# Loading the first chunk tile by tile in the order of use, with wider warming products

## The chip, the cores and the metric

One core of one Trainium2 chip runs the kernel once per measurement. The metric is the device time of one execution in microseconds (us), as the median of several runs; smaller is better. All times below that are given with a start count from the first instruction of the profiled execution.

## The reference

One transformer block on x of 256 rows and 1024 features, all in 32-bit floats. What matters here is its beginning:

```
h    = rms_norm(x, norm_mix_g)             # x: 256 x 1024
proj = h @ w_in                            # 1024 x 2048: k, q, v and u of 512 columns each
k, q = rope(rms_norm(k, g)), rope(rms_norm(q, g))
x    = x + concat(pool(u), attention(q, k, v)) @ w_out
x    = x + cross_attention(norm(x), norm(mem)) @ ...     # reads mem, 256 x 1024
x    = x + conv_ffn(norm(x))                             # w_up 1024 x 5632, w_down 2816 x 1024
```

## The kernel before

x lies transposed on the chip: eight tiles (k = 0 to 7) of 128 features x 256 rows, in the tile `sc` (columns C_X on; `resid` is a view of them). All weights come through one stream, `wpack`, in chunks of 128 x 2048 floats (1 MB). A chunk holds two units of 1024 columns, and a ring of three buffers `raw` takes the chunks in turn. In the first part each unit holds two 512-column weight tiles, so that chunk 0 (called W0 below) has the weights of k = 0 to 3 of the first product, chunk 1 (W1) those of k = 4 to 7; W2 and W3 hold the next product (q), W4 and W5 the one after it (v), and so on. The first block of `wpack`, W0, is stored so that each quarter of 512 columns is contiguous in memory; of W1 and later chunks each partition has a row of 8 KB, and a load of some columns takes a piece of every row. x is stored as one contiguous block for each load (`FIRST_X` lists the cuts).

Every product is made of three passes on TensorE, because each number is split in a high part (float32r, a rounding by ACT or DVE) and a low part (the rest, by DVE): `wh` and `wl` of the weights (L207, L218), `xg` high and low of the scaled x (L268, L274). `a_chunk` runs k = 0 to 7 for one product of 512 columns: for each k, two matmuls of 512 columns at L408 (high x, high weight), two at L410 (low x, high weight) and two at L413 (high x, low weight). `first_splits` writes out by hand the order of the splits for the first product:

```
for k in range(KT):
    if k == 2: split_h(k // 2, r)                      # weight's high part first
    part_h(xgv[0][:, k], resid[:, k], col(sc, C_GMIX + k))
    if k != 2: split_h(k // 2, r, dve.tensor_copy if k == 0 else act.copy)
    part_l(...); split_l(...)
```

Engines work off their instructions in the order in which the program gives them. Later units are split by `need`, some units ahead of TensorE; `loads_to` issues a chunk's load on SP's queue when the buffer that it takes (the one of three chunks before) has been read by the last split of it, DVE's `wl`. Between these, by hand-tuned numbers of waiting steps (the WAIT lists), jobs place the rest: squares of x and their sum (`sqx`, `accx`), rope of k and q (L425 to L457), the transposes of k and q (L489, L493), scores (L567), softmax (L596), the pool branch (L682 to L685). The eight matmuls at L366, before all this, multiply zeros into a PSUM bank that nobody reads; they are the warming products.

The first loads are issued on SP's queue, but for the first half of W0, which is issued on ACT's. The loads share eight semaphores in rotation: from the ninth load on, the issuing queue waits for the landing of the load eight places before.

Of the kernel before, what the change touches and what calls it, by code (L numbers as in the profile page):

```python
# [9 lines left out]
F32 = mybir.dt.float32  # L10
F32R = mybir.dt.float32r
# [5 lines left out]
P = 128  # L17
D = 1024
S = 256
KT = D // P  # L20
# [47 lines left out]


C_GMIX, C_X = 0, KT  # L70
FIRST_X = [0] + [C_X + k * S for k in (1, 2, 4, 6, 8)]
FIRST_W = [0, 512, 1024, 1536, 2048]
C_GMEM, C_GX, C_GFFN = (C_X + KT * S + 8 * i for i in range(3))
C_GXQ = C_GFFN + KT
# [13 lines left out]
def block_kernel(ctx: ExitStack, tc: tile.TileContext, wpack: bass.AP, xpack: bass.AP, scal: bass.AP,  # L88
                 memT: bass.AP, table: bass.AP, out: bass.AP):
    nc = tc.nc  # L90
    pe, act, dve, pool = nc.tensor, nc.scalar, nc.vector, nc.gpsimd
# [11 lines left out]
    def bank():  # L103
        turn[0] += 1
        return psum.tile([P, 512], F32, name=f"bank{turn[0]}", tag="bank", bufs=8)
# [59 lines left out]
    def block(flat, lo, hi):  # L165

        return flat[P * lo:P * hi].rearrange("(p n) -> p n", p=P)

    def load_chunk(c, cuts=(0, 2 * UNIT), queue=nc.sync):
        raw[c] = wring.tile([P, 2 * UNIT], F32, name=f"raw{c}", tag="raw", bufs=RAW)  # L170
        for lo, hi in zip(cuts, cuts[1:]):
            load_part(c, lo, hi, queue)
        next_load[0] = c + 1

    def load_part(c, lo, hi, queue=nc.sync):
        src = wpack[c, :, lo:hi]
        if c == 0:
            src = block(wpack[c].rearrange("p n -> (p n)"), lo, hi)
        queue.dma_start(raw[c][:, lo:hi], src)
# [19 lines left out]
    def split_h(u, r=slice(0, UNIT), copy=act.copy):  # L199
        if u // 2 == MISC:  # L200
            for j in range(2 * (u % 2), 2 * (u % 2) + 2):
                misc[j] = maskr[:, 2 * P:] if j == 2 else t2(f"misc{j}", F32R)
                act.copy(misc[j], unit(u)[:, 512 * (j % 2):512 * (j % 2) + 512])
            return
        if u not in split:
            split[u] = [wring.tile([P, UNIT], F32R, name=f"wh{u}", tag="wh", bufs=LOOK + 3), None]
        copy(split[u][0][:, r], unit(u)[:, r])  # L207

    def split_l(u, r=slice(0, UNIT)):
        if u // 2 == MISC:  # L210
            if u % 2 == 1:
                misc["l"] = t2("misc_l", F32R)
                dve.tensor_tensor(misc["l"], unit(u)[:, 512:], misc[3].bitcast(F32), op=ALU.subtract)
            return
        if split[u][1] is None:
            split[u][1] = wring.tile([P, UNIT], F32R, name=f"wl{u}", tag="wl", bufs=LOOK + 2)
        h, l = split[u]
        dve.tensor_tensor(l[:, r], unit(u)[:, r], h[:, r].bitcast(F32), op=ALU.subtract)  # L218
# [45 lines left out]
    def part_h(h, src, scale=None):  # L264
        if scale is None:
            act.copy(h, src)
        else:
            act.activation(h, src, AF.Copy, scale=scale)  # L268

    def part_l(l, src, h, scale=None):  # L270
        if scale is None:
            dve.tensor_tensor(l, src, h.bitcast(F32), op=ALU.subtract)
        else:
            dve.scalar_tensor_tensor(l, src, scale, h.bitcast(F32), op0=ALU.mult, op1=ALU.subtract)  # L274
# [28 lines left out]
    def col(t, c):  # L303
        return t[:, c:c + 1]
# [53 lines left out]
    def load_x(lo, hi):  # L358
        r = slice(C_X + lo * S if lo else 0, C_X + hi * S)
        nc.sync.dma_start(sc[:, r], block(xpack, r.start, r.stop))  # L360

    ones = nc.const_aps.tensor(1.0, (P, 1), F32)
    idle = nc.const_aps.tensor(0.0, (P, P), F32)
    warm = bank()
    for _ in range(WARM):
        pe.matmul(warm[:, 0:P], idle, idle, start=True, stop=True)  # L366

    load_x(0, 1)
    load_chunk(0, (0, 512), nc.scalar)
    load_part(0, 512, 1024, nc.scalar)  # L370
    load_x(1, 2)
    load_part(0, 1024, 1536)
    load_x(2, 4)
    load_part(0, 1536, 2048)
    load_x(4, 6)
    load_chunk(1, (0, 1024))
    load_x(6, 8)
    load_part(1, 1024, 2048)
    load_chunk(2, (0, 1024, 2048))
    nc.sync.dma_start(tab, table)  # L380
    nc.sync.dma_start(sc[:, C_GMEM:], scal)
# [2 lines left out]
    def first_splits():  # L384
        for k in range(KT):
            r = slice(k % 2 * 512, k % 2 * 512 + 512)

            if k == 2:
                split_h(k // 2, r)
            part_h(xgv[0][:, k], resid[:, k], col(sc, C_GMIX + k))  # L390
            if k != 2:
                split_h(k // 2, r, dve.tensor_copy if k == 0 else act.copy)
            part_l(xgv[1][:, k], resid[:, k], xgv[0][:, k], col(sc, C_GMIX + k))
            split_l(k // 2, r)
        next_split[0] = FIRST

    first_splits()

    def a_chunk(u0, actv, bk, *first):
# [746 lines left out]
```

## Time and profile before

| | |
|---|---|
| median of 3 runs (lowest, highest) | 381.89 us (381.72, 381.90) |
| the profiled execution's own time | 382.99 us |
| its span, first to last instruction | 381.2 us |
| PE, DVE, ACT, POOL busy | 376.5, 315.1, 246.8, 67.8 us |
| mean granted TensorE clock | 0.999 |

The profiled execution takes 1.1 us more than the median of the others, and 1.8 us of its time lie around the span. PE's 376.5 us are the times that its matmuls cover; they overlap in the pipeline, so a busy PE need not be at its fastest. A row of the timeline gives start, length, engine, line, what is written from what, and in brackets the idle time before with what ended it; "PEld" is the weight load of TensorE.

### The profile page before, as it was taken

The page shows a single profiled execution, that of the slowest core. Times are in us where ns is not written, and L with a number is a line of the kernel's source. Part 1 is how long each engine was busy: PE and PEld are TensorE (multiplying, and loading weights), DVE is VectorE, ACT ScalarE, POOL GpSimd, SP SyncE. Part 2 cuts the span into 40 slices and gives each one's busy share as a digit, 9 for nine tenths or more (in the row PEclk, how much of TensorE's full clock was granted, in tenths as well). Part 3 has the DMA queues.
Part 4 walks back from the last instruction along what each step waited for, and adds up shares of the span by engine and source line. Part 5 has one row for each costly group of instructions (what it writes and reads, how often), then busy time and mean ns, then how long its engine had stood idle before and what let it go on. Part 6 is the DMA issues. An engine that isn't in the chain of part 4 may idle for free.

```text
span 381.2 us, 6011 instructions
## 1 busy us (share of the span) xinstructions
PE 376.5 (99%) x2194; PEld 328.6 (86%) x2194; DVE 315.1 (83%) x570; ACT 246.8 (65%) x471; POOL 67.8 (18%) x148
## 2 busy tenths in 40 slices
PE   9999999999999999999999999999999999999996
PEld 7788888888888988898888888888888888888896
DVE  4689999979878859778979999999999998654460
ACT  5766878976557655845655588778877777442210
POOL 0252885142831212100220000000000000000000
PEclk9999999999999999999999999999999999999999
DMA  8996382453506635352536155665555654374500
GB/s 263 422 369 223 111 329 67 170 208 119 216 0 220 222 110 209 123 222 111 179 124 251 55 181 208 221 219 200 179 192 207 219 168 165 124 249 157 200 15 28
DMA packets 12412, 69.13 MB, mean 181 GB/s; under 512 B 1376, under 2 KB 2784, under 8 KB 4832
## 3 DMA queue, kind: packets, MB, share of 16 engines
q1 hardware_dynamic: 12096, 68.24, 49.9%
q10 hardware_dynamic: 288, 0.52, 0.4%
q8 instruction: 17, 0.28, 0.3%
q14 instruction: 11, 0.09, 0.1%
HBM read 67.71 MB, written 1.05 MB: 180 GB/s over the span
## 4 chain that ended last, share of the span: by engine, by line
PE 86%; DVE 5%; DMA 4%; POOL 2%; ACT 1%; issue 1%; ACTq 0%; DVEq 0%
PE bank L301 42%; PE bank L300 22%; PE bank L408 4%; PE bank L413 4%; PE bank L410 4%; DMA raw<-wpack 4%; DVE wl L218 2%; PE bank L285 2%; PE bank L283 2%; PE bank L284 2%; PE bank L606 1%; PE bank L567 1%; PE bank L738 0%; PE bank L876 0%; POOL rs1t L248 0%
## 5 line engine op out<-in xcount | busy, mean ns | idle before, releaser
L218 DVE TENSOR_TENSOR wl<-raw,wh 128x1024 fp32r<-128x1024 f32 (+1 forms) x127 | 151.0, 1205 | 4.5 <-ACT wh L207 4.3
L207 ACT CAST wh<-raw 128x1024 fp32r<-128x1024 f32 (+1 forms) x125 | 126.1, 1028 | 39.1 <-DMA raw<-wpack 24.1
L301 PE MATMUL bank<-hs,wh 128*128 128x512 f32 x304 | 105.4, 391 | 0.0
L300 PE MATMUL bank<-hs,wl 128*128 128x256 f32 x304 | 85.2, 280 | 0.0
L301 PEld LDWEIGHTS bank<-hs,wh 128*128 128x128 f32 x304 | 56.9, 187 | 12.4
L300 PEld LDWEIGHTS bank<-hs,wl 128*128 128x128 f32 x304 | 57.5, 189 | 0.0
L301 PE MATMUL bank<-act,wh 128*128 128x512 f32 x154 | 53.4, 391 | 0.0
L300 PE MATMUL bank<-act,wl 128*128 128x256 f32 x154 | 43.1, 280 | 0.0
L991 ACT ACTIVATE y<-up,sc 128x256 f32<-128x256 f32 x44 | 26.2, 602 | 22.3 <-DVE up L978 17.8
L301 PE MATMUL bank<-h,wh 128*128 128x512 f32 x112 | 39.4, 394 | 0.0
L998 DVE SCALAR_TENSOR_TENSOR y<-up,sc,y 128x255 f32<-128x255 f32 (+1 forms) x88 | 37.0, 494 | 0.0
L301 PEld LDWEIGHTS bank<-act,wh 128*128 128x128 f32 x154 | 28.8, 187 | 6.3
L300 PE MATMUL bank<-h,wl 128*128 128x256 f32 x112 | 31.8, 284 | 0.0
L300 PEld LDWEIGHTS bank<-act,wl 128*128 128x128 f32 x154 | 29.1, 189 | 0.0
L1045 DVE TENSOR_TENSOR o<-bank,sc 128x256 f32<-128x256 f32 x8 | 3.4, 425 | 28.3 <-PE bank L301 22.4
L301 PEld LDWEIGHTS bank<-h,wh 128*128 128x128 f32 x112 | 21.0, 188 | 4.5
L301 PE MATMUL bank<-cat,wh 128*128 128x512 f32 x62 | 21.8, 393 | 0.0
L301 PE MATMUL bank<-ox,wh 128*128 128x512 f32 x62 | 21.6, 394 | 0.0
L268 ACT ACTIVATE h<-sc 128x256 fp32r<-128x256 f32 x16 | 8.2, 510 | 20.3 <-DVE sc L784 20.2
L300 PEld LDWEIGHTS bank<-h,wl 128*128 128x128 f32 x112 | 21.2, 189 | 0.0
L408 PE MATMUL bank<-wh,xg 128*128 128x512 f32 x64 | 20.4, 400 | 0.5 <-ACT wh L207 0.5
L408 PE MATMUL bank<-wh,mg 128*128 128x512 f32 x64 | 20.6, 403 | 0.0
(249 smaller groups left out, 718.3 us busy)
## 6 DMA issues: line engine op xcount, KB each, us to landing
raw<-wpack SPq DMA_DIRECT2D x59, 1024.0 KB, 4.8
raw<-wpack SPq DMA_DIRECT2D x4, 512.0 KB, 7.9
mraw<-memT SPq DMA_DIRECT2D x4, 256.0 KB, 8.2
out<-o SPq DMA_DIRECT2D x8, 128.0 KB, 1.9
sc<-xpack SPq DMA_DIRECT2D x3, 256.0 KB, 4.9
raw<-wpack ACTq DMA_DIRECT2D x2, 256.0 KB, 3.4
raw<-wpack SPq DMA_DIRECT2D x2, 256.0 KB, 4.4
tab<-table SPq DMA_DIRECT2D x1, 480.0 KB, 9.3
```

The lines of the kernel that those rows point to most:

```text
L207: copy(split[u][0][:, r], unit(u)[:, r])
L218: dve.tensor_tensor(l[:, r], unit(u)[:, r], h[:, r].bitcast(F32), op=ALU.subtract)
L268: act.activation(h, src, AF.Copy, scale=scale)
L283: pe.matmul(o, stat[0], mov[0], start=start, stop=False)
L284: pe.matmul(o, stat[0], mov[1], start=False, stop=False)
L300: pe.matmul(b[:, 0:n], stat[1], mov[:, 0:n], start=start, stop=False, skip_group_check=not wide_first)
L301: pe.matmul(b, stat[0], mov, start=False, stop=stop, skip_group_check=not wide_first)
L408: pe.matmul(bk[tt], a[tt][0], wv[0], start=k == 0, stop=False)
L410: pe.matmul(bk[tt], a[tt][1], wv[0], start=False, stop=False)
L413: pe.matmul(bk[tt], a[tt][0], wv[1], start=False, stop=k == KT - 1)
L991: act.activation(y[:, g * S:(g + 1) * S], src[:, g * S:(g + 1) * S], AF.Identity, bias=col(sc, C_CB + f), scale=col(sc, C_CW + 2 * 2 * NFF ...
L998: dve.scalar_tensor_tensor(yy[:, j:], uu[:, :S - j], col(sc, C_CW + (2 - j) * 2 * NFF + f), yy[:, j:], op0=ALU.mult, op1=ALU.add)
```

## The change

The x tiles 2 to 7, which came in three loads of two tiles, come in six loads of one tile. W1, which came in two loads of 1024 columns, comes in four of 512. The loads of x and W1 alternate in the order in which the first product uses them. For k = 3, as for k = 2 before, ACT makes the weight's high part ahead of x's. The warming products become 512 columns wide and float32r, where they were 128 columns of float32; there are eight of them as before.

```diff
-FIRST_X = [0] + [C_X + k * S for k in (1, 2, 4, 6, 8)]
+FIRST_X = [0] + [C_X + k * S for k in range(1, KT + 1)]
...
-    idle = nc.const_aps.tensor(0.0, (P, P), F32)
+    idle = nc.const_aps.tensor(0.0, (P, 512), F32).bitcast(F32R)
     warm = bank()
     for _ in range(WARM):
-        pe.matmul(warm[:, 0:P], idle, idle, start=True, stop=True)
+        pe.matmul(warm, idle[:, 0:P], idle, start=True, stop=True)
 
     load_x(0, 1)
     load_chunk(0, (0, 512), nc.scalar)
     load_part(0, 512, 1024, nc.scalar)
     load_x(1, 2)
     load_part(0, 1024, 1536)
-    load_x(2, 4)
+    load_x(2, 3)
     load_part(0, 1536, 2048)
-    load_x(4, 6)
-    load_chunk(1, (0, 1024))
-    load_x(6, 8)
-    load_part(1, 1024, 2048)
+    load_x(3, 4)
+    load_x(4, 5)
+    load_chunk(1, (0, 512))
+    load_x(5, 6)
+    load_part(1, 512, 1024)
+    load_x(6, 7)
+    load_part(1, 1024, 1536)
+    load_x(7, 8)
+    load_part(1, 1536, 2048)
     load_chunk(2, (0, 1024, 2048))
...
-            if k == 2:
+            if k in (2, 3):
                 split_h(k // 2, r)
             part_h(xgv[0][:, k], resid[:, k], col(sc, C_GMIX + k))
-            if k != 2:
+            if k not in (2, 3):
                 split_h(k // 2, r, dve.tensor_copy if k == 0 else act.copy)
```

SP's queue from the third x load on, before (`sc<-xpack` is x, `raw_88` W0, `raw_96` W1, `raw_100` W2, `raw_157` W3; in brackets the semaphores that the issue waits for, DMAHW0 to 7 being the eight that rotate):

```order
L360 DMA sc<-xpack 128x512
L179 DMA raw_88<-wpack 128x512
L360 DMA sc<-xpack 128x512
L179 DMA raw_96<-wpack 128x1024 [waits DMAHW0_49]
L360 DMA sc<-xpack 128x512 [waits DMAHW1_49]
L179 DMA raw_96<-wpack 128x1024 [waits DMAHW2_49]
L179 DMA raw_100<-wpack 128x1024 [waits DMAHW3_49]
L179 DMA raw_100<-wpack 128x1024 [waits DMAHW4_49]
L380 DMA tab<-table 128x960 [waits DMAHW5_49]
L381 DMA sc<-scal 128x208 [waits DMAHW6_49]
L179 DMA raw_157<-wpack 128x2048 [waits DMAHW7_49,DVE_49]
```

The same place after the change (`raw_97` is W1, `raw_105` W2):

```order
L360 DMA sc<-xpack 128x256
L179 DMA raw_88<-wpack 128x512
L360 DMA sc<-xpack 128x256
L360 DMA sc<-xpack 128x256 [waits DMAHW0_49]
L179 DMA raw_97<-wpack 128x512 [waits DMAHW1_49]
L360 DMA sc<-xpack 128x256 [waits DMAHW2_49]
L179 DMA raw_97<-wpack 128x512 [waits DMAHW3_49]
L360 DMA sc<-xpack 128x256 [waits DMAHW4_49]
L179 DMA raw_97<-wpack 128x512 [waits DMAHW5_49]
L360 DMA sc<-xpack 128x256 [waits DMAHW6_49]
L179 DMA raw_97<-wpack 128x512 [waits DMAHW7_49]
L179 DMA raw_105<-wpack 128x1024 [waits DMAHW0_49]
```

Five more loads stand ahead of W2 and W3 on SP's queue. They carry the same bytes, and W2, the tables and W3 follow in the order in which they stood.

ACT's queue at the first splits (`xg` is the high part of an x tile, `wh` that of a weight tile), the difference:

```order
 L268 ACTIVATE xg<-sc 128x256 x2
-L207 CAST wh_107<-raw_88 128x512
-L207 CAST wh_116<-raw_88 128x512
+L207 CAST wh_112<-raw_88 128x512
+L207 CAST wh_121<-raw_88 128x512
+L268 ACTIVATE xg<-sc 128x256
+L207 CAST wh_121<-raw_88 128x512
 L268 ACTIVATE xg<-sc 128x256 x2
-L207 CAST wh_116<-raw_88 128x512
+L207 CAST wh_132<-raw_97 128x512
```

Only the splits of k = 3 change places there; DVE's and PE's instructions keep their order.

## Rows read from the trace of the kernel before

**Rows 1.** The page: busy times, and the chain that ended last.
```profile
PE 376.5 (99%) x2194; PEld 328.6 (86%) x2194; DVE 315.1 (83%) x570; ACT 246.8 (65%) x471; POOL 67.8 (18%) x148
PE 86%; DVE 5%; DMA 4%; POOL 2%; ACT 1%; issue 1%; ACTq 0%; DVEq 0%
```

**Rows 2.** Timeline, PE, first product (x2: two matmuls in the row).
```profile
4.42 0.80 PE L408 MATMUL bank<-wh,xg 128*128 128x512 f32 x2
5.07 0.63 PE L410 MATMUL bank<-wh,xg 128*128 128x512 f32 x2
5.53 0.62 PE L413 MATMUL bank<-wl,xg 128*128 128x512 f32 x2
...
9.85 0.61 PE L413 MATMUL bank<-wl,xg 128*128 128x512 f32 x2
10.96 0.74 PE L408 MATMUL bank<-wh,xg 128*128 128x512 f32 x2 [0.49 <-ACT wh L207]
...
16.57 0.61 PE L408 MATMUL bank<-wh,xg 128*128 128x512 f32 x2
```

**Rows 3.** The chain of work up to 110 us, in order of time: start, length, what.
```profile
3.84 6.42 DMA raw<-wpack
10.29 0.63 ACT wh L207
10.96 0.74 PE bank L408 x2
...
14.92 0.45 PE bank L413 x2
...
21.73 1.49 DVE wl L218
...
45.53 1.23 DVE wl L218
46.77 6.72 DMA raw<-wpack
```

**Rows 4.** Timeline, ACT: its first wait for W3.
```profile
18.77 1.05 ACT L207 CAST wh<-raw 128x1024 fp32r<-128x1024 f32 x1 [1.58 <-DMA raw<-wpack]
20.65 1.99 ACT L207 CAST wh<-raw 128x1024 fp32r<-128x1024 f32 x2
```

**Rows 5.** Timeline, DVE.
```profile
19.85 1.68 DVE L218 TENSOR_TENSOR wl<-raw,wh 128x1024 fp32r<-128x1024 f32 x1 [2.46 <-ACT wh L207]
21.72 1.49 DVE L218 TENSOR_TENSOR wl<-raw,wh 128x1024 fp32r<-128x1024 f32 x1 [0.19 <-PE bank L410]
```

**Rows 6.** Busy time by stretch: us, PE, PEld, DVE, ACT, POOL busy, PE's clock, DMA share, GB/s.
```profile
21.70:46.70 25.00, 25.00 (x122) 20.93 (x121) 24.16 (x44) 17.59 (x30) 12.92 (x28) 1.00 0.61 227
46.70:54.60 7.90, 7.90 (x46) 6.34 (x45) 7.83 (x14) 5.60 (x12) 6.86 (x17) 1.00 0.84 309
```

**Rows 7.** Timeline, PE and its weight loads, where PE waits again.
```profile
47.52 0.41 PEld L567 LDWEIGHTS bank<-qkT 64*128 64x128 f32 x6 [0.36 <-ACT mg L268]
57.13 0.28 PE L684 MATMUL bank<-maskr,uh 128*128 128x256 f32 x1
57.41 0.39 PE L685 MATMUL bank<-maskr,ul 128*128 128x256 f32 x1
57.63 0.28 PE L682 MATMUL bank<-misc,uh 128*128 128x256 f32 x1
57.75 0.28 PE L683 MATMUL bank<-misc,ul 128*128 128x256 f32 x1
59.03 0.99 PE L558 MATMUL bank<-maskr,identr 128*128 128x256 f32 x4
59.95 2.06 PE L567 MATMUL bank<-qkT 64*128 64x128 f32 x32
```

**Rows 8.** DMA rates by stretch (columns as in rows 6, the last is GB/s).
```profile
0.00:3.00 3.00, 2.25 (x10) 2.27 (x11) 0.00 (x0) 1.28 (x1) 0.19 (x4) 1.00 0.40 104
4.60:6.00 1.40, 1.40 (x7) 1.14 (x8) 1.40 (x4) 1.28 (x3) 0.00 (x0) 1.00 1.04 363
6.00:7.00 1.00, 1.00 (x6) 0.84 (x5) 0.27 (x1) 0.58 (x2) 0.00 (x0) 1.00 1.07 369
7.00:9.00 2.00, 2.00 (x10) 1.26 (x9) 1.78 (x4) 1.51 (x4) 0.00 (x0) 1.00 0.88 257
9.50:13.00 3.50, 3.01 (x14) 2.14 (x13) 2.27 (x6) 2.71 (x6) 0.00 (x0) 1.00 1.03 421
20.00:22.00 2.00, 2.00 (x10) 1.66 (x9) 1.81 (x2) 2.00 (x5) 1.92 (x2) 1.00 1.03 383
3.00:3.50 0.50, 0.50 (x5) 0.50 (x4) 0.00 (x0) 0.00 (x0) 0.00 (x0) 1.00 1.05 381
```

**Rows 9.** DMA issues of short windows: first x; W1's first half (3.84); W3 (9.33).
```profile
sc<-xpack SPq DMA_DIRECT2D x1, 132.0 KB, 2.8
raw<-wpack SPq DMA_DIRECT2D x1, 512.0 KB, 6.4
raw<-wpack SPq DMA_DIRECT2D x1, 1024.0 KB, 9.4
```

**Rows 10.** The warming products (L366) and the first product's loads (L410): ns min/median/max.
```profile
L366 PEld LDWEIGHTS bank<-const-float32-0.0 x16: 288/333/334, 0.7 to 3.9; 128*128 128x128 f32 x16
L410 PEld LDWEIGHTS bank<-wh,xg x14: 187/188/189, 4.8 to 14.3; 128*128 128x128 f32 x14
```

**Rows 11.** Timeline: the warming products, DVE's first split, SP's queue up to W3.
```profile
0.76 3.75 PE L366 MATMUL bank<-const-float32-0.0 128*128 128x128 f32 x16 [0.76 <-PEq L1138]
3.85 0.43 DVE L207 CAST wh<-raw 128x512 fp32r<-128x512 f32 x1 [3.85 <-DMA raw<-wpack]
4.69 1.70 SPq L179 DMA_DIRECT2D raw<-wpack  x3
8.62 0.69 DVE L218 TENSOR_TENSOR wl<-raw,wh 128x512 fp32r<-128x512 f32 x1
9.33 5.65 SPq L179 DMA_DIRECT2D raw<-wpack  x2
```

## The prediction

> **What bounds the kernel now.** I read the page first: PE covers 99% of the span and is 86% of the chain that ended last [rows 1], so a microsecond that PE saves counts only if nothing else holds PE back later. So I looked at the start, which is what the change touches, and then followed the chain until PE carries it alone.
>
> At the start PE's pairs of 512-column matmuls follow each other every 0.455 us (5.53 less 5.07 is 0.46; the chain's later pieces are 0.45) [rows 2, 3]. One k takes three pairs, 1.365 us, and eight of them 10.92 us. From its first matmul at 4.42 to the second product's at 16.57 PE takes 12.15 us [rows 2]. So it loses 1.23 us. Of that 0.2 go to the first pair (5.07 less 4.42 is 0.65) [rows 2]. The largest piece is at k = 4: from 9.85 the next pair should have started at 10.31, it started at 10.96, because ACT split W1's first half only at 10.29, when its 512 KB landed, 6.4 us after the issue [rows 2, 3, 9]. That is 0.65 us; the other 0.4 lie in gaps of about 0.1 at k = 2, 3 and 4.
>
> The chain then leaves PE: from 21.73 to 46.77 it runs over DVE (with POOL's small steps in it) and then over a weight load [rows 3]. DVE is busy 24.16 of 25.00 us from 21.7 to 46.7 and 7.83 of the next 7.90 [rows 6], so DVE sets the pace there, and PE only seems full. What started this full stretch? DVE sat idle 2.46 us until 19.85 for ACT's split of W3, and ACT 1.58 us until 18.77 for W3's landing [rows 4, 5]. The next split of DVE, at 21.72, begins where ACT's second split of W3 ends (20.65 plus about 1.0) [rows 4, 5]. So the landing of W3 sets when DVE's work begins, and W3 lands 9.4 us after its issue [rows 9], because the transfers ahead of it fill the DMA engines.
>
> PE meets this work again at 47.52, where it waits 0.36 us for ACT's copies of q and k; at 57.41, where the step is 0.28 instead of 0.12 us; and at L558, where 59.03 to 59.95 takes 0.92 instead of 0.46 us for four matmuls of 256 columns [rows 7]. That makes 0.36 + 0.16 + 0.46 = 0.98 us of waiting. A PE that comes 1 us earlier waits 1 us longer there.
>
> **The change part by part.** Loads in order. W1's first quarter now ends the first 1.97 MB that are loaded (W0, x 0 to 4 and itself), where W1's first half ended 2.36 MB (W0, x 0 to 5 and itself): 0.39 MB less, which is 1.0 us at 369 to 383 GB/s [rows 8]. So it lands near 9.2, and earlier if the slow stretch below is shorter; ACT's split (0.63 [rows 3]) ends at 9.9. PE, no longer held at k = 2 and 3, wants it at 4.42 + 0.2 + 4 x 1.365 = 10.1. The later quarters come about 1.0 us apart (0.39 MB each), against PE's 1.365. So the first product runs without a gap and ends 1.0 us earlier, near 15.6. ACT's swap at k = 3 costs nothing: both its splits are done before PE's k = 3 at 8.7.
>
> This microsecond PE gives back at 47.52 to 59.95, if the work it waits for there does not come earlier too. That work hangs on W3's landing, so the term that counts is how W3 moves:
> 1. Rows of 2 KB instead of 4 KB for W1. The stretch 9.5 to 13.0 moves mostly 4 KB rows at 421 GB/s, 20 to 22 mostly 2 KB rows of mem at 383 [rows 8]. 1.05 MB take 2.74 instead of 2.49 us: +0.25.
> 2. Rows of 1 KB instead of 2 KB for x, 0.79 MB. The only stretch with many 1 KB rows (3.0 to 3.5) also holds W0 and shows 381, no less than the 363 and 369 of the 2 KB stretches behind it [rows 8]. So 0 at best; at worst another 10% of 2.1 us, +0.2. I take +0.1.
> 3. The slow stretch. From 7.0 to 9.0, when W1's first half moves, the rate is 257 instead of 369 [rows 8]: 0.22 MB, 0.6 us lost. No row says why. If it belongs to that one 512 KB load of strided rows, it may vanish (-0.6); if a quarter of half the size loses half, -0.3; if W1's first load keeps it, 0. I take -0.3.
> 4. Five more issues on SP, about 0.43 to 0.57 us each (three take 1.70) [rows 11]. 18 of them end near 9, and W3's issue at 9.33 waits for DVE's split of k = 3, which ends at 9.31 [rows 11]: hidden. With eight loads in flight there are now about 1.5 MB queued, 4 us at 380 GB/s, against 2.8 us for a first load with an empty queue [rows 9], so the engines stay fed, with 1.2 us to spare.
>
> Sum: 0.25 + 0.1 - 0.3 = +0.05 us, that is nothing; between 0.25 - 0.6 = -0.35 and 0.25 + 0.2 = +0.45.
>
> The Trainium skill speaks against the smaller loads: "Perfetto Trace Analysis", DMA Optimizations, says that small DMAs (under 2 KB) have much per-transfer overhead and that batching can raise throughput dramatically. By it the 1 KB rows of x would cost more than term 2; the trace so far shows 10% from 4 KB to 2 KB and nothing clear below.
>
> Warming products. Sixteen records take 3.75 us, to 4.51 at the latest, and PE's first real work waits for DVE's split, 3.85 + 0.43 = 4.28 [rows 11]. A 512-column float32r matmul is what the main loop runs, at 0.2275 us. The granted clock prints 1.00, the higher of the two levels, from the first stretch on [rows 8], yet a weight load of the same size takes 333 ns in the warming and 188 after it [rows 10]. So I read the warming as run at the lower level, and take up to twice 0.2275. Eight then need 1.8 to 3.64 us and end at 2.6 to 4.4: no delay, since 4.42 is the start now. Cost 0.
>
> The profiled execution's span would be 381.2 + 0.05 and its time 383.0; the median of the runs lies 1.1 below the profiled time, and the same difference on it gives 381.9.
>
> **The rivals.** (a) PE's gain is kept: W3 lands almost a microsecond earlier, or DVE's full stretch is not what PE waits for. For it: the slow stretch could go and with it some lateness of single DMA engines that no row shows; PE is 86% of the chain [rows 1]. Against it: DVE's 24.16 of 25.00 us [rows 6] and the waits [rows 7]. Price: up to -1.0, 380.9.
>
> (b) The alternation spoils the transfers: each quarter of W1 meets the slow stretch, as every one of them again starts the strided rows after a contiguous x tile. Half the loss each, 4 x 0.3 instead of 0.6, gives +0.6; the full loss each, +1.8. With terms 1 and 2 (+0.35) W3 lands 0.95 to 2.15 later, and DVE, then PE, with it, since PE's 0.98 us of waiting sit behind DVE. Middle +1.3, 383.2. It decides from the point at which W3 lands over 0.8 later, near 19.5. Against it: W1's second half came after an x load too and falls in the stretch at 421 [rows 8]. The Trainium skill's "DMA: Bandwidth & Descriptors", Latency and other measured facts, has slow copies where rows lie a large power of two apart (512 KiB and more); W1's rows lie 8 KB apart, so no run here shows that it applies.
>
> (c) The wide products run over: above 0.455 us each they hold back the first product. At 0.7 each they end at 6.4, PE starts 2.0 late; 1.0 is recovered by the closed gaps and 0.98 by the waits, so about 0. Only from 0.85 on does it show +1 or more: 383. A related case: they end at 2.6, PE idles to 4.4, and the clock stays at or returns to the lower level; eight us of first product at twice 0.455 cost 4, less 2: 383.9. Nothing in the rows prints a lower clock.
>
> **How the numbers follow.** Likeliest, gain given back: 0.62, 381.9 (own range 381.5 to 382.4). (a) 0.18. (b) 0.14. (c) both together 0.06. About 0.2% (0.76 us) is what a measurement can tell from no change. Faster is (a) and a tail: 0.19; slower (b), (c) less their milder part: 0.18; same 0.63. The range takes (a) whole, from 380.9, and of (b) the milder half, to 382.9, which leaves out some 0.15.
>
> **What would show it.** Right: W1's quarters land one by one with the first before 9.5; PE has no wait at k = 4 and starts the second product near 15.6; W3's first split by ACT starts within 0.5 us of 18.77; PE waits about a microsecond more at 47 to 60. Wrong: DVE's split at 21.72 moves by 0.8 or more either way; PE's first matmul after 4.6; a stretch under 300 GB/s that lasts beyond 10 us; or PE 1 us early at 60, which would mean that the chain through DVE was not the one that binds.

## The result, and the profile after

The changed kernel takes 384.22 us (median of 6 runs, 383.26 to 384.98), the kernel before 381.96 beside it (6 runs, 381.72 to 382.39): a ratio of 1.0051 [1.0039, 1.0063]. It is slower by half a per cent, and outside the range of the forecast. The ratios here and below leave out one execution each of e6 (967 us), e13 (760 us) and e17 (1923 us), far from all others; the medians hold them. The profiled execution takes 384.98 us with a span of 383.0, 1.8 us more than that of before; it is the longest of the six, so its landings are likely later than those of a middle execution (e1, below, has most of the loss with W3 at 20.08). The lines of the changed kernel lie five further down: L413, L415 and L418 are the three passes that were L408, L410 and L413.

The page of the changed kernel, to set against [rows 1]: PE's busy time is much the same, and its part of the chain that ended last falls from 86 to 83%.

```profile
PE 377.4 (99%) x2186; PEld 327.4 (85%) x2186; DVE 314.7 (82%) x570; ACT 247.1 (65%) x471; POOL 67.3 (18%) x148
PE 83%; DVE 7%; DMA 4%; ACT 2%; issue 2%; POOL 2%; SPq 0%; DVEq 0%; ACTq 0%
```

The timeline of the changed kernel, PE with its weight loads, then ACT, DVE and SP's queue, to set against [rows 2, 4, 5, 7, 11]:

```profile
0.72 3.06 PEld L366 LDWEIGHTS bank<-const-float32-0.0 128*128 128x128 f32 x8 [0.72 <-issue]
0.76 3.75 PE L366 MATMUL bank<-const-float32-0.0 128*128 128x512 f32 x8 [0.76 <-PEq L1143]
4.43 0.70 PE L413 MATMUL bank<-wh,xg 128*128 128x512 f32 x2
...
6.84 0.62 PE L418 MATMUL bank<-wl,xg 128*128 128x512 f32 x2
8.10 0.73 PE L413 MATMUL bank<-wh,xg 128*128 128x512 f32 x2 [0.65 <-ACT xg L268]
...
10.70 0.62 PE L418 MATMUL bank<-wl,xg 128*128 128x512 f32 x2
11.16 0.62 PE L413 MATMUL bank<-wh,xg 128*128 128x512 f32 x2
...
16.14 0.61 PE L418 MATMUL bank<-wl,xg 128*128 128x512 f32 x2
16.98 0.73 PE L413 MATMUL bank<-wh,xg 128*128 128x512 f32 x2 [0.23 <-ACT wh L207]
...
48.77 0.41 PEld L572 LDWEIGHTS bank<-qkT 64*128 64x128 f32 x6 [0.67 <-ACT qkT L498]
...
7.02 0.62 ACT L207 CAST wh<-raw 128x512 fp32r<-128x512 f32 x1 [1.53 <-DMA raw<-wpack]
9.41 0.62 ACT L207 CAST wh<-raw 128x512 fp32r<-128x512 f32 x1
13.99 0.62 ACT L207 CAST wh<-raw 128x512 fp32r<-128x512 f32 x1 [1.20 <-DMA raw<-wpack]
15.88 1.05 ACT L207 CAST wh<-raw 128x1024 fp32r<-128x1024 f32 x1 [0.95 <-DMA raw<-wpack]
21.17 1.05 ACT L207 CAST wh<-raw 128x1024 fp32r<-128x1024 f32 x1 [1.71 <-DMA raw<-wpack]
...
22.25 1.35 DVE L218 TENSOR_TENSOR wl<-raw,wh 128x1024 fp32r<-128x1024 f32 x1 [2.77 <-ACT wh L207]
24.13 1.23 DVE L218 TENSOR_TENSOR wl<-raw,wh 128x1024 fp32r<-128x1024 f32 x1 [0.53 <-ACT wh L207]
...
5.17 0.43 SPq L179 DMA_DIRECT2D raw<-wpack  x1
7.01 0.33 SPq L360 DMA_DIRECT2D sc<-xpack  x1
7.39 0.43 SPq L179 DMA_DIRECT2D raw<-wpack  x1
11.68 4.01 SPq L179 DMA_DIRECT2D raw<-wpack  x2
```

Read it in this order. PE starts at 4.43 (4.42 before) and has no gap at k = 4 (10.70, 11.16), where it waited before. But it waits at k = 2: W0's third quarter landed at 7.00 (ACT's split at 7.02), 5.61 before. ACT's splits at 13.99 (W1's last quarter), 15.88 (W2's first half) and 21.17 (W3) all wait for a landing. W3's first split by ACT starts 2.4 us later than at 18.77 [rows 4], and DVE's split of W3's second half at 24.13, 2.41 after 21.72 [rows 5]. From there DVE is busy 24.15 of 25.00 us (24.1 to 49.1, below), as it was before [rows 6], and PE meets its work late: at L572 its weight loads wait 0.67 us until 48.77, where they waited 0.36 until 47.52 [rows 7]. SP issued W3's load at 11.68, 2.35 us later than at 9.33 [rows 11].

Busy time by stretch of the changed kernel (columns as in [rows 6, 8]):

```profile
4.60:6.00 1.40, 1.40 (x7) 1.05 (x7) 1.40 (x4) 0.89 (x2) 0.00 (x0) 1.00 0.90 320
7.00:9.00 2.00, 1.35 (x6) 0.62 (x5) 0.92 (x2) 1.98 (x5) 0.00 (x0) 1.00 1.02 347
9.50:13.00 3.50, 3.50 (x17) 2.87 (x17) 3.50 (x8) 3.00 (x6) 0.00 (x0) 1.00 0.82 254
13.00:15.50 2.50, 2.50 (x13) 2.07 (x12) 1.28 (x3) 0.94 (x2) 0.00 (x0) 1.00 0.96 338
24.10:49.10 25.00, 24.76 (x124) 20.39 (x123) 24.15 (x44) 17.74 (x31) 12.93 (x29) 1.00 0.60 218
```

The slow stretch is not at 7 to 9 any more (347 against 257 GB/s), it is at 9.5 to 13, where 421 GB/s stood before and now 254 do, with the DMA engines busy 0.82 of the time.

No view of the page shows what the landing records of the trace do: each load has sixteen, which the text reads as one for each DMA engine. For W1's last load and for W3, the first, the eighth and the last of the sixteen (us):

```
kernel                      W1's last load          W3
before                   11.10  11.48  12.17   17.68  18.03  18.74
changed                  11.48  11.92  13.97   18.65  19.76  21.15
x in pairs (e10)         11.32  11.95  12.34   17.92  18.51  18.88
tiles 2, 3 alone (e16)   11.12  11.43  13.68   18.19  19.02  20.39
one pair cut (e20)       10.88  11.40  12.96   17.56  17.95  19.51
W1 in eighths (e21)      10.93  11.17  12.16   17.85  18.27  19.53
```

In the four kernels that lose time (all but before and e10) the middle engine brings W1's end within half a microsecond of before, but the last is 1.2 to 2.6 us behind the first, where 1.07 was the spread before (W3: 1.7 to 2.5, and 1.06). The reader of a load waits for the last engine. At W3 that engine is the whole loss only in some: the middle one is late by -0.08 of the last one's 0.77 us in e20 and by 0.24 of 0.79 in e21, but by 1.73 of 2.41 in the changed kernel and by 0.99 of 1.65 in e16. There half of the engines or more fell behind, not one.

### The profile page after: what moved, and what is told of

The parts are those of the page before. It is cut to its first block, busy times and chain, and to the rows that moved or that the text cites. A ratio compares the mean times of both kernels' runs of the same rounds, so it can differ in the third digit from the quotient of the medians.

```text
span 383.0 us, 6004 instructions
## 1 busy us (share of the span) xinstructions
PE 377.4 (99%) x2186; PEld 327.4 (85%) x2186; DVE 314.7 (82%) x570; ACT 247.1 (65%) x471; POOL 67.3 (18%) x148
## 4 chain that ended last, share of the span: by engine, by line
PE 83%; DVE 7%; DMA 4%; ACT 2%; issue 2%; POOL 2%; SPq 0%; DVEq 0%; ACTq 0%
PE bank L301 41%; PE bank L300 22%; DMA raw<-wpack 4%; PE bank L418 4%; PE bank L413 3%; PE bank L415 3%; DVE wl L218 2%; PE bank L285 2%; PE bank L284 2%; PE bank L283 2%; PE bank L611 1%; DVE mg L274 1%; ACT wh L207 1%; PE bank L572 1%; PE bank L743 0%
## 5 line engine op out<-in xcount | busy, mean ns | idle before, releaser
L413 PE MATMUL bank<-wh,xg 128*128 128x512 f32 x64 | 20.4, 400 | 0.9 <-ACT xg L268 0.7
L413 PE MATMUL bank<-wh,mg 128*128 128x512 f32 x64 | 20.7, 405 | 0.0
```

The source lines that it names most:

```text
L413: pe.matmul(bk[tt], a[tt][0], wv[0], start=k == 0, stop=False)
```

## The experiments

Each was timed in five rounds beside the kernel before. A loss in microseconds is the ratio less one times 382; the changed kernel's is 1.9. About 0.2 us of each such loss lies outside the span: the time is 1.8 us longer than the span in the kernel before, e2, e8, e10, e11, e13, e15 and e19, and 2.0 us longer in the changed kernel and all the other runs, which are those with loads cut to 128 KB; why is not shown. "W3 at" is the start of ACT's first split of W3 in the profile of that run. Theory A: the loads come later and with them W3, and that is the loss. Theory B: the warming products cost it. Theory A1 has the gapped rows of W1 and W2 as the reason why the loads come later, theory A2 the many short loads.

**The two halves of the change.** e1_loads_only is the changed kernel with the old warming products, e2_warm_only the kernel before with the new ones.

```diff
-    idle = nc.const_aps.tensor(0.0, (P, P), F32)
+    idle = nc.const_aps.tensor(0.0, (P, 512), F32).bitcast(F32R)
...
-        pe.matmul(warm[:, 0:P], idle, idle, start=True, stop=True)
+        pe.matmul(warm, idle[:, 0:P], idle, start=True, stop=True)
```

> The changed kernel with the old warming products (128 columns, float32); only the loads and the order of two splits differ from before. Theory A (the loads ahead of W3 move more slowly, W3 lands some 2 us late, and DVE's full stretch with it): as slow as the changed kernel, 383.8 to 384.5 us, W3's split by ACT at 20.5 to 21.5. Theory B (the wide warming products cost it): back to 381.9 us.

> The kernel before with the wide warming products alone. Theory A: 381.9 us, no change, W3's split by ACT at 18.7, first matmul at 4.4. Theory B: 383.5 to 384.5 us.

Measured: e1 383.9, ratio 1.0040 [1.0027, 1.0052], W3 at 20.08; e2 382.16, ratio 0.9997 [0.9988, 1.0005], W3 at 18.27. Theory B falls. W3 comes half a microsecond sooner in e2 than in the profile of before (18.77), with the same loads: so far apart can two profiles be.

**W1's rows.** e3_w1_blocks stores each of W1's quarters as one block (of W2 too in e6_w12_blocks); e4_w1_halves loads W1 in halves, with x still tile by tile.

```diff
-        if c == 0:
+        if c in BLOCKED:                  # e3: 0 and 1 in quarters; e6: also 2 in halves
             src = block(wpack[c].rearrange("p n -> (p n)"), lo, hi)
...
-    load_chunk(1, (0, 512))               # e4, W1's other quarters likewise
+    load_chunk(1, (0, 1024))
```

> The changed kernel with W1's four quarters each stored contiguously, as W0's are; the same loads in the same order and number. Theory A1 (pieces of rows that lie 8 KB apart are what is read slowly): W1 moves at 360 GB/s or more, W3 lands 1 to 2 us sooner than in the changed kernel, 382.0 to 383.0 us; W2's halves are still pieces of rows, so some of the loss can stay. Theory A2 (many small loads with eight in flight: SP waits for the landing of a late one and the queue runs dry): no change, 384.2 us, the rate from 8.5 to 11.5 stays below 300 GB/s.

> The changed kernel with W1 in two halves as before (x 4 and x 5, then the first half, x 6 and x 7, then the second); x stays in single tiles. Theory A1: one slow stretch as before (0.6 to 1 us), 382 to 383 us. Theory A2: two loads fewer, a part of the loss is back, 383 us or more. If small rows are the cause: W1's rows are 4 KB again, 382.5 us.

> The changed kernel with W1's quarters and W2's halves each stored as one contiguous block, so that no load ahead of W3 reads rows with gaps between them; the count, the sizes and the order of the loads are the changed kernel's. Theory A1 (the loss is the gapped rows of W1 and W2, 8 KB apart): W3 lands between 18.2 and 18.7 us, as in the kernel before, and the time is 382.0 to 382.5. Theory A2 (the loss is the many small loads in turns, whatever their layout): W3 lands at 19.5 or later and the time stays at 383.4 to 384.2.

Measured: e3 383.65, 1.0032 [1.0023, 1.0042], W3 at 19.33. e4 384.19, 1.0045 [1.0031, 1.0059], W3 at 20.54. e6 383.0, 1.0023 [1.0011, 1.0035], W3 at 19.85. Contiguous W1 wins back 0.7 us, W2 with it 1.1, and the larger loads of W1 no more than the measurement can tell (e3's interval just overlaps that of the changed kernel, e6's does not). So A1 can hold for half; 0.9 us are left with no gapped row ahead of W3.

**W3 or the table first.** If W3's landing sets the time, moving the table and scal behind it should gain: e8_before_tab_later does so in the kernel before, e9_after_tab_later in the changed one.

```diff
-    nc.sync.dma_start(tab, table)
-    nc.sync.dma_start(sc[:, C_GMEM:], scal)
...
-    side_loads = {5: load_mem}
+    side_loads = {4: load_tab, 5: load_mem}    # load_tab: the two loads above
```

> The kernel before, with the two loads of constants (the table, 480 KB, and scal, 104 KB) issued behind W3 and no longer ahead of it; nothing else moves. If W3's landing sets the time, as the explanation has it: the two loads took 1.49 us of the transfers (14.76 to 16.25), so W3 lands near 17.25 and the time falls by 0.8 times that, to 380.9 or 381.0. If the late landing only goes along with something else that costs the time: W3 lands near 17.25 too, and the time stays at 382.1 within 0.3.

> The changed kernel with the table and scal behind W3. If W3's landing sets the time: W3 lands 1.5 us earlier than without (20.05 and 21.15 in two profiles of these loads), near 19.1, and the time falls from 384.1 to 382.9. Otherwise it stays at 383.8 to 384.3.

Measured: e8 381.9, 0.9998 [0.9989, 1.0006]; e9 384.1, 1.0055 [1.0035, 1.0076]. No gain, though W3 came earlier. As I had put it, the theory missed this; the timeline of e9, ACT and DVE, shows why:

```profile
18.95 1.05 ACT L207 CAST wh<-raw 128x1024 fp32r<-128x1024 f32 x1 [0.24 <-DMA raw<-wpack]
...
23.03 1.06 ACT L207 CAST wh<-raw 128x1024 fp32r<-128x1024 f32 x1 [1.15 <-DMA raw<-wpack]
23.98 1.08 ACT L453 ACTIVATE sqk<-bank 128x512 f32<-128x512 f32 x2
...
21.91 1.23 DVE L218 TENSOR_TENSOR wl<-raw,wh 128x1024 fp32r<-128x1024 f32 x1 [0.65 <-PE bank L417]
24.61 1.29 DVE L454 TENSOR_TENSOR m1k<-bank,ropek 128x512 f32<-128x512 f32 x2 [0.52 <-ACT sqk L453]
```

W3 is split at 18.95, but the next split in ACT's order is W4's, which waits until 23.03, and the squares of k stand behind it on ACT; DVE waits for those. W4 lies behind the table whichever way the two are ordered, so it lands when it landed (its last engine at 22.93 in e9, 22.58 in e1, 23.69 in the changed kernel). DVE's full stretch starts with the last of these, and it is the sum of all bytes ahead of W4 that counts, with the lateness of the engines.

**Short loads.** e10_x_pairs loads x in pairs again and keeps the rest, W1's quarters in the order of use among them. e13_x_1kb_rows is e10 with each pair read as two blocks of 1 KB rows by one load. e14_x_half_rows has the 18 loads of the changed kernel with rows of 2 KB: each loads 64 partitions of a pair.

```diff
-    load_x(2, 3)                          # e10, tiles 4 to 7 likewise
+    load_x(2, 4)
     load_part(0, 1536, 2048)
-    load_x(3, 4)
...
+        src = xpack[P * r.start:P * r.stop].rearrange("(k p n) -> p k n", k=2, p=P)        # e13
+        nc.sync.dma_start(sc[:, r].rearrange("p (k n) -> p k n", k=2), src)
...
+        nc.sync.dma_start(sc[p, r], block(xpack, r.start, r.stop)[p])                      # e14
```

> The changed kernel with x's tiles 2 to 7 loaded in pairs again (2 KB rows) and W1 still in quarters in the order of use: 15 loads ahead of the table in place of 18. Theory A2 in the form that the single tiles of x cost it: W3 lands near 18.9 and the time is 382.3 to 382.8. Theory A1 (W1's quarters cost it): W3 lands at 19.8 or later and the time stays at 383.6 to 384.2.

> As the kernel with x's tiles 2 to 7 in pairs and W1 in quarters (which took 382.4, W3 landing at 18.88), but each pair read as two blocks of 1 KB rows by one load: the rows of the changed kernel's single tiles without its three more loads. Theory A2r (the loss is the 1 KB rows): W3 lands at 19.8 or later and the time is 383.5 to 384.2. Theory A2n (the loss is the number of loads, 18 ahead of the table in place of 15): W3 lands by 19.1 and the time stays at 382.2 to 382.7.

> The changed kernel with the same 18 loads of the same sizes at the same places in the queue, but each pair of x's tiles is loaded as 64 of its partitions and then the other 64, in rows of 2 KB, in place of one tile and then the other in rows of 1 KB. Theory A2r (1 KB rows): W3 lands by 19.2 and the time is 382.2 to 382.9. Theory A2n (the number of loads): W3 lands at 19.8 or later and the time stays at 383.5 to 384.2.

Measured: e10 382.39, 1.0009 [1.0000, 1.0017], W3 at 18.90; e13 382.57, 1.0010 [1.0001, 1.0019], W3 at 19.47; e14 384.2, 1.0053 [1.0040, 1.0066], W3 at 20.19. So W1's quarters cost about 0.3 us, with an interval that starts at nothing, rows of 1 KB by themselves nothing that shows in the time (e13's W3 lies between its two forecasts), and the single tiles of x the other 1.6. In e14 no engine falls far behind (W3's first and last landing are 0.7 apart), but it is late in another way, as this stretch shows (columns as in [rows 6, 8]; first e14):

```profile
5.00:13.00 8.00, 6.69 (x29) 4.74 (x28) 5.39 (x11) 4.52 (x10) 0.00 (x0) 1.00 1.06 278
```

and the same stretch of e10:

```profile
5.00:13.00 8.00, 8.00 (x34) 6.50 (x33) 6.48 (x14) 6.33 (x13) 0.00 (x0) 1.00 1.02 342
```

The engines are busy all the time in both, but move 278 in place of 342 GB/s. So e14, whose loads are 128 KB too, proves nothing for the number of loads.

**How many short loads, and where.** e16_x23_alone has only tiles 2 and 3 single, e17_x47_alone only 4 to 7, e18_x_then_w1 has all single tiles ahead of W1. e20_before_x23_apart is the kernel before with one pair cut in two at its place. e21_w1_eighths has x in pairs and W1 in eight contiguous loads of 128 KB.

```diff
-    load_x(4, 5)                          # e16, tiles 6 and 7 likewise; e17: tiles 2 and 3
+    load_x(4, 6)
...
+    load_x(5, 6)                          # e18: ahead of W1's first quarter
+    load_x(6, 7)
+    load_x(7, 8)
...
-    load_x(2, 4)                          # e20, against the kernel before
+    load_x(2, 3)
+    load_x(3, 4)
...
-    load_part(1, 512, 1024)               # e21, W1's other quarters likewise
+    load_part(1, 512, 768)
+    load_part(1, 768, 1024)
```

> The changed kernel with only x's tiles 2 and 3 loaded singly, around W0's last quarter; tiles 4 and 5, and 6 and 7, in pairs again: 16 loads ahead of the table. If each more load costs its part: a third of the way from the version with all pairs (382.4) to the changed kernel (384.1), 383.0. If the place among W1's quarters is what costs: 382.2 to 382.6, W3 landing by 19.0.

> The changed kernel with tiles 2 and 3 as a pair again and tiles 4 to 7 still single, in turns with W1's quarters: 17 loads ahead of the table. If each more load costs its part: 383.5. If the place among W1's quarters is what costs: 383.8 to 384.3, W3 landing at 19.8 or later.

> The changed kernel's 18 loads with x's tiles 4 to 7 all ahead of W1's four quarters, not in turns with them. If the taking in turns costs the time: 382.2 to 382.9 and W3 landing by 19.1. If the number of short loads costs it, or the few bytes that eight loads in flight hold: 383.6 to 384.3 and W3 at 19.8 or later.

> The kernel before with x's tiles 2 and 3 as two loads of 128 KB, one right behind the other at the pair's place; nothing else differs. If a short load costs as such (theory A2s): 383.2 to 384, W3 landing at 19.5 or later in the profile. If it costs only in the changed kernel's order, with W0's last quarter between the two: 381.8 to 382.3.

> The version with x in pairs and contiguous W1 and W2 (381.9), with W1 cut into eight contiguous loads of 128 KB in place of four of 256 KB, in the same order: 19 loads ahead of the table. If a short load costs as such (theory A2s): 383 to 384, with single engines a microsecond or more behind the others. If only x's tiles do it: 381.8 to 382.4.

Measured: e16 383.84, 1.0050 [1.0033, 1.0067], W3 at 20.41. e17 383.49, 1.0041 [1.0025, 1.0058], but from 382.4 to 385.8; its profile is that of a 382.4 execution, W3 at 18.82. e18 384.12, 1.0058 [1.0046, 1.0070], W3 at 19.94. e20 383.94, 1.0044 [1.0031, 1.0056], W3 at 19.53. e21 383.72, 1.0043 [1.0030, 1.0057], W3 at 19.55. Neither the place, nor the taking in turns, nor a part for each load explains these: one pair of x cut in two costs 1.7 us, four more single tiles on top (e18) at most half a microsecond more, and weights cut to 128 KB cost the same. The timeline of e20, ACT and PE, then DVE:

```profile
11.03 0.62 ACT L207 CAST wh<-raw 128x512 fp32r<-128x512 f32 x1 [2.37 <-DMA raw<-wpack]
11.70 0.73 PE L409 MATMUL bank<-wh,xg 128*128 128x512 f32 x2 [0.89 <-ACT wh L207]
...
19.53 1.05 ACT L207 CAST wh<-raw 128x1024 fp32r<-128x1024 f32 x1 [1.55 <-DMA raw<-wpack]
22.49 1.50 DVE L218 TENSOR_TENSOR wl<-raw,wh 128x1024 fp32r<-128x1024 f32 x1 [0.18 <-ACT wh L207]
```

W1's first half, whose load nothing has changed, lands at 11.01 in place of 10.26, so that the gap at k = 4 grows (0.89 in place of 0.49, in brackets here and in [rows 2]), and W3 follows. The mean rate did not fall (stretches of e20, columns as in [rows 6, 8], to set against 257 and 421 GB/s there):

```profile
7.00:9.00 2.00, 2.00 (x10) 1.66 (x9) 1.82 (x4) 1.64 (x4) 0.00 (x0) 1.00 0.95 267
9.50:13.00 3.50, 2.61 (x12) 1.83 (x11) 1.48 (x4) 1.97 (x5) 0.00 (x0) 1.00 1.03 415
```

**A faster version.** e11_before_tab_w12 is the kernel before with contiguous halves of W1 and W2 and the later table; e15_pairs_tab_w12 is e10 with contiguous W1 and W2 and the later table; e19_pairs_w12 is e15 with the table ahead of W3 again. The edits are those shown above.

> The kernel before with W1's and W2's halves stored as contiguous blocks and the table and scal behind W3. If DVE's full stretch starts with the last of W3 and the table, whichever that is: the order of the two changes nothing (as the run with the table behind W3 alone had it, 381.9), and only what the contiguous halves save counts, 0.3 to 0.5 us off the last landing (18.30 for the table in that run) and up to 0.65 at k=4 of the first product: 381.4 to 381.8. If the contiguous halves save nothing here: 381.9 to 382.2.

> x in pairs, W1 in quarters in the order of use, W1's quarters and W2's halves contiguous, the table and scal behind W3, wide warming products: what the runs so far speak for. If x in pairs is what keeps the engines together and the last landing starts DVE's full stretch: the last of W3 and the table lands near 18.1 and the time is 381.3 to 381.8. If W1's quarters or the contiguous blocks set single engines back also with x in pairs: the last landing is at 19 or later and the time 382.3 to 383.

> The faster version (381.57) with the table and scal ahead of W3 again: x in pairs, W1 in contiguous quarters, W2 in contiguous halves, wide warming products. If DVE's stretch starts with the later of W3 and the table, their order is worth nothing: 381.4 to 381.8. If the later table is part of the gain: 381.9 to 382.3.

Measured: e11 382.07, 1.0000 [0.9991, 1.0008], so the contiguous halves saved nothing there (its profile, 383.81, is its longest execution: one engine brought W0's third quarter at 7.64, the fifteenth at 5.98); e15 381.57, 0.9987 [0.9978, 0.9995]; e19 381.9, 0.9998 [0.9990, 1.0007]. e15 beats both kernels, by half a microsecond over the kernel before, with an interval that just stays below one. Whether the later table has a part in it the intervals of e15 and e19 don't settle, since they overlap. The timeline of e15, ACT:

```profile
16.82 1.05 ACT L208 CAST wh<-raw 128x1024 fp32r<-128x1024 f32 x1 [0.21 <-DMA raw<-wpack]
20.91 1.06 ACT L208 CAST wh<-raw 128x1024 fp32r<-128x1024 f32 x1 [1.16 <-DMA raw<-wpack]
```

W3 is split at 16.82 and W4 at 20.91, 2.1 us before the 23.03 of e9.

## Why the prediction was wrong

**What binds: right.** The forecast had W3's landing start DVE's full stretch, and PE meet it again at 47 to 60. Over the sixteen profiles of kernels that keep the table ahead of W3, the span follows W3:

| kernel | W3 at | span |
|---|---|---|
| e19, e2 | 18.00, 18.27 | 380.1, 380.5 |
| before, e17, e10 | 18.77, 18.82, 18.90 | 381.2, 380.4, 380.6 |
| e3, e13, e20, e21 | 19.33, 19.47, 19.53, 19.55 | 381.1, 381.0, 381.4, 381.5 |
| e6, e18, e1, e14 | 19.85, 19.94, 20.08, 20.19 | 381.6, 381.8, 381.8, 382.2 |
| e16, e4 | 20.41, 20.54 | 382.0, 382.2 |
| changed | 21.17 | 383.0 |

From 19.33 to 21.17 the span grows by 1.9 for 1.84, a microsecond for each. Below 18.9 it gains less, 0.5 from 18.90 to 18.00. The price that rival (b) set on a late W3, and its deciding point near 19.5, were about right. The table is a correlation, and moving W3 alone on purpose gave nothing (e8, e9), because W4's split stands behind it on ACT. So the stretch is started by W3 or W4, whichever keeps ACT longer, and that part the prediction didn't have.

A point behind both waits takes in all the profiles, those with the later table too. DVE runs the same 570 instructions in the same order in every one of them. The timeline at its first L261, in the order before, e10, changed, e9, e8:

```profile
34.44 0.36 DVE L261 TENSOR_SCALAR hk<-ssk,ex 128x8 f32<-128x8 f32 x2 [0.35 <-POOL ex L327]
34.45 0.36 DVE L261 TENSOR_SCALAR hk<-ssk,ex 128x8 f32<-128x8 f32 x2 [0.35 <-POOL ex L327]
36.59 0.37 DVE L261 TENSOR_SCALAR hk<-ssk,ex 128x8 f32<-128x8 f32 x2 [0.35 <-POOL ex L327]
35.61 0.37 DVE L261 TENSOR_SCALAR hk<-ssk,ex 128x8 f32<-128x8 f32 x2 [0.35 <-POOL ex L327]
33.63 0.36 DVE L261 TENSOR_SCALAR hk<-ssk,ex 128x8 f32<-128x8 f32 x2 [0.35 <-POOL ex L327]
```

Against e10 (span 380.6) the changed kernel is 2.14 us later there and 2.4 at the end, e9 1.16 and 1.4 (span 382.0). e8 is 0.82 earlier there and 0.2 at the end (380.4), e15 1.23 and 0.7 (33.22, at L262; 379.9). So a later start of the stretch is paid in full, and an earlier one gives back a part. The profile of before alone is out of line: it loses 0.6 us more behind this point than e10.

**PE's first product: half right.** W1's first quarter was to land near 9.2 and ACT's split to end at 9.9; it landed at 9.38, the split ended at 10.03, and the gap at k = 4 went. But the second product started at 16.98, not near 15.6. Of that, 0.8 us are the new gap at k = 2 (8.10 where 6.84 and 0.455 give 7.30), from W0's third quarter, whose load the change had not touched, and about 0.3 the slower passes behind it (8.10 to 9.79 for one k). And 0.38 are W2's first half, landing at 15.86: 16.14 and 0.455 give 16.60. The prediction had followed W1 and W3 and put nothing on W2.

**Terms 1 and 2: small, as said.** W1's quarters cost 0.3 us in e10, where term 1 had 0.25 on W3 (its split starts at 18.90, against 18.77 before and 18.27 in e2). The 1 KB rows cost less than 0.1 between e10 and e13 by their ratios (1.0009, 1.0010); term 2 had 0.1.

**Term 3: this step failed.** It was to take 0.3 off W3 because the slow stretch would lose half with loads of half the size. The slow stretch moved and grew: 3.5 us at 254 in place of 2 us at 257 GB/s, and W3 landed 2.4 us later in this profile, 1.3 in e1. Both are signs that the prediction had set for being wrong (DVE's split at 21.72 moved by more than 0.8, a stretch under 300 GB/s lasted beyond 10 us). So the sum of +0.05 for W3's landing should have been +1.3 to +2.4, above even the bound of +0.45, and the range, which took only the milder half of rival (b), ended at 382.9. The larger fault is what the sum left out. It had no term for a short load as such: term 2 priced x's rows, term 4 the added issues, the one at 0.1 and the other at nothing. e20 cuts one pair of x, leaves W1's loads as they were and loses 1.7 us, and its slow stretch is that of before (267 and 415 GB/s, where 257 and 421 stood). There the last engine is late, and no mean rate shows it.

**Term 4: the margin was no margin.** Eight loads in flight were to keep the engines fed with 1.2 us to spare. That takes the sixteen engines as level. The last of W0's third quarter came at 7.00, so SP, which waits for the load eight places before, issued x's tile 6 only at 7.01 and W1's third quarter at 7.39. That quarter's first engine landed at 10.28, 2.9 us later, about what a first load of 256 KB takes with an empty queue (2.7, from 0.71 to 3.44 in the kernel before). So the early engines seem to have run dry, which fits the DMA share of 0.82 from 9.5 to 13. W3's own late issue, at 11.68, cost nothing: its first engine landed 2.5 us behind that of the load ahead of it (16.13, 18.65), which is 1 MB at some 420 GB/s, so nothing was waited for. In e1 the profile has no such delay of W0 (its last engine at 5.64), and e1 loses 1.5 us where the changed kernel loses 1.9, so this step is not needed for most of the loss.

**Rival (b): right in size, wrong in its reason.** It had the quarters of W1 meet the slow stretch one after the other because they alternate with contiguous tiles. With W1 contiguous (e3) 1.2 us of loss remain, with no alternation (e18) all of it, with alternation but x in pairs (e10) almost none. Rival (a) did not happen: PE gained nothing that it kept. Rival (c) falls with e2. In the changed kernel the eight wide products took the 3.75 us that sixteen narrow ones had taken [rows 11], to 4.51, just past the upper end of what was forecast for them (4.4): they start 0.43 us apart, where the main loop has 0.2275, though the granted clock prints 1.00 (the higher level) there too. PE started where it did before, at 4.43.

**Short rows and short loads.** The prediction set the Trainium skill's rule on small DMAs ("Perfetto Trace Analysis", DMA Optimizations) aside because the rows showed little for short rows. The runs bear out its direction for a load as a whole, far above 2 KB, and not for its rows: a cut to 128 KB costs 1.7 us (e20), 1 KB rows in a load of 256 KB hardly anything (e13 against e10). The same section of the Trainium skill says that splitting may let work start sooner if DMA engines are generally idle; here the DMA share was 0.88 to 1.07 from 4.6 us on [rows 8], so its condition wasn't met. Why one late engine holds everything, the Trainium skill says in "DMA: Bandwidth & Descriptors", Why a DMA increments its semaphore by 16 and not by 1: the engines of one DMA finish independently, and only the full count of 16 means that all has landed. The landing records agree (12.96 the last, 11.40 the eighth in e20).

**What stays open.** Why a load of 128 KB sets single engines back is not shown. x's tiles 0 and 1 are short in every kernel, those that lose nothing too. The number of loads ahead of the table does not order the times (13 and 15 lose little, 14, 16, 18 and 19 most, 17 varies from execution to execution; up to 16 it is the even counts that lose, which the 19 of e21 speaks against), but that some place in the rotation of the eight semaphores matters is not excluded. Each kernel has one profile, and the engine that is late, and where, differs between them. e11, whose x comes in pairs, has one as late as any in its profile, so short loads may make late engines more frequent and not be their only source.

## What to carry to other kernels

Where the DMA engines are full, cutting a load to have its first part sooner can be paid by every load behind it (x's tiles of 128 KB were, W1's quarters of 256 KB hardly): look up which far landing starts the next full stretch (here W3's and W4's, 20 us on) before looking at the near one. Price a load by its last engine too, not by the mean rate alone: one late engine in sixteen moves every wait behind it. When a landing is moved earlier, read on the waiting engine's own queue what it waits for next.

## What the runs showed of the hardware

- Loads of 256 KB cut to 128 KB (128 partitions of 1 KB) in the first microseconds cost: one pair cut in two 1.7 us of the whole (e20), and two such loads about as much as six or eight (e16, e18, e21). A load of 512 KB cut to 256 KB costs little (e10, 1.0009 [1.0000, 1.0017]). The same 1 KB rows in loads of 256 KB cost no more than e10's 2 KB rows (1.0010 and 1.0009).
- DMA engines drift apart: the sixteen landings of one load lie 1.1 us apart in the kernel before and 2.5 in the changed one, and most of the drift is kept over the next loads (W1's last load and W3: 2.49 and 2.50; e20 2.08 and 1.95).
- Contiguous rows in place of rows 8 KB apart for W1 and W2 gave 1.1 us where engines had drifted (e6, ratio 1.0023 for 1.0051) and 0.4 with x in pairs (e19 and e10, 0.9998 for 1.0009, intervals that overlap); in the kernel before with the later table they gave nothing (e11 and e8, 1.0000 and 0.9998).
